# A hybrid decoder trunk on one core: the planner's model of DMA queue and landings, larger transposed pieces of the latents, and four staging sets at attention's end

## The chip, the cores and the metric

The kernel runs on one core of a Trainium2 chip. The core has a matrix engine (TensorE, called PE in the profile; its weight loads, PEld, run beside the matmuls), a vector engine (DVE), a scalar engine (ACT), GpSimd (POOL) and a sync engine (SP). Each engine works through its own instructions in the order in which they stand in the program, and waits at an instruction until its operands are there. Here SP and POOL issue the transfers, each in order, and sixteen DMA engines move the data. The metric is device time in microseconds (us), lower is better.

## What is computed

Two layers over 2048 tokens of 1024 channels: a Mamba-2 mixer, then multi-head latent attention (MLA) with 16 heads, each with a residual, and a last norm over the rows.

```python
def reference(x, positions, ...):
    h = x + mamba2_mixer(rms_norm(x, g_pre[0]), ...)
    cos, sin = rope_tables(positions)
    ckv, k_rope = split(rms_norm(h, kv_g_in) @ kv_w_down, [256])
    k_nope, v = split(rms_norm(ckv, kv_g_latent) @ kv_w_up)
    cq, gate = split(rms_norm(h, g_pre[1]) @ mla_w_in, [384])
    q = rms_norm(cq, mla_g_q) @ mla_w_uq
    o = causal_block_attention(q_nope, rope(q_rope), k_nope, rope(k_rope), v)
    h = h + (o * silu(gate)) @ mla_w_out
    return rms_norm(h, g_final)
```

`ckv` and `cq` are the latents: 256 key-value and 384 query numbers per token, normed and projected up again.

## The kernel before

Tokens are worked in four blocks of 512 (TB), channels in slices of 128 (KD = 8 of them in 1024). Operands of a product are split into two fp16 halves, high and low, and each product is three matmuls into the same PSUM bank (`mm3`, L904 to L906: high by high, high by low, low by high); only the first block of the Mamba layer works in fp32 forms. A "split" below is the pair of instructions that makes the halves: ACT writes the high half, DVE the low one.

**Stage 1, both layers' projections (`layers`, 0 to about 1930 us).** The Mamba layer goes through four blocks of four groups each: input projections, scan, output projection. The MLA part goes block by block through the latents (`mla_kv_down`, `mla_cq`), the gate (`mla_gate`) and the up-projections (`mla_up`), and beside that prepares the next block's normed input xT (`prep16`), by DMA transposes out of a split tile (xT<-wsp). All instructions of this stage are first recorded by a `Score` and then put in order by its planner, `plan`: `forward` simulates the engines, taking at each moment the ready instruction of highest rank; `backward` works out from that schedule how late each may start, which gives the next ranks. This is repeated PLANS times, the shortest schedule is kept, and `play` emits the instructions in the order of their planned starts. All of them so carry one line in the profile, L878. For a DMA the planner has a time of issue and a time to landing (`cost`); for copies the old `forward` also keeps a clock of the transfers in flight (`dma`) and adds LATE, while a transposing DMA lands in a flat 3300 ns and does not hold that clock. The plan fixes order only; real waits are on semaphores. Since DVE, ACT and SP are in order, an instruction whose operand lands late holds whatever stands behind it.

**The latents.** `latent` evicts the product's four banks (128 tokens each) into xs and norms them; `turned` splits each into yt and has SP transpose it in pieces of 128 channels, high and low half together (128x2x128): two pieces per 128 tokens for the key-value latents, into tiles BC, three for the query latents, into tiles yT. DVE then scales each channel slice (BC<-BC, yT<-yT) for the up-projections. The scaling of xT by xg is of the same kind.

**Stage 2, attention (`heads`, about 1930 to 2612 us).** 64 pieces n = 0 to 63, four query blocks in each of the 16 heads. `Pace`, a second planner with its own costs and tables of ranks, orders softmax and products. At its end it starts on the output projection of the first token block: for channel slice k, step G loads attention output, gate and reciprocal row sums into one of GATED staging sets (four DMAs), H multiplies them on DVE, I (ACT) and J (DVE, L2327) make the two halves, and P is the product. ASKED says at which n which slices are loaded.

**Stage 3, the output stage (`back`, 2612 us to the end).** The rest of the output projection, ordered by the framework's scheduler. For block b and slice k, `gated` loads the same three operands into a buffer "os" (three of them), DVE multiplies (L2260, L2262), ACT and DVE split the product into oT (L2466, L2467), and PE multiplies it by W. Products are added to the residual rows h (L2481); when a half block's rows are complete, `final` norms them, scales them by the final gain gf (four instructions of L2487) and writes them out.

## Time and profile before

| | us |
|---|---|
| median of 3 runs | 2784.39 (2779.01 to 2787.86) |
| the profiled execution | 2791.74 |
| its span in the trace | 2789.9 |
| PE's last matmul ends | 2781.0 |

The profile is of one execution, so sums of its durations are made against 2791.74 us, and the span is what its timeline shows. A row of a timeline gives start, length, engine, line, operation, output and inputs, how many like instructions it groups, and in brackets how long the engine stood idle before it and what ended that. A view of waits adds such idle times up by pair. "Granted clock" is the share of full speed that PE was allowed.

### The profile page before, as it was taken

To read this page: it belongs to the slowest core of one execution; us is meant where nothing else is said; L and a number is where in the kernel's file an instruction comes from. 1 tells how busy PE (TensorE), PEld (TensorE's weight loads), DVE (VectorE), ACT (ScalarE), POOL (GpSimd) and SP (SyncE) were. 2 spreads that over 40 slices of the span, in tenths; PEclk is the share of its full clock that TensorE was granted. 3 is DMA by queue.
4 is the path that set the end of the run, shared out by engine and by line. 5 is a ranking of instruction groups with operands and counts; after the bars stand their busy time and mean duration, and the time that the engine had idled before them with its cause. 6 is when DMAs were issued, how large, how long until landed. Compare 5 with 4: busy or idle time off the path is not lost. (4 is left out here: it accounts for less than half of the span.)

```text
span 2789.9 us, 48569 instructions
## 1 busy us (share of the span) xinstructions
PE 2737.9 (98%) x16120; PEld 1550.7 (56%) x16120; DVE 2220.0 (80%) x5048; ACT 1864.2 (67%) x4914; POOL 675.6 (24%) x832
## 2 busy tenths in 40 slices
PE   7999999999999999999999999999999999999998
PEld 6888766554555555555555545454555555555443
DVE  5889899999988879888786564646889888889676
ACT  6889877877776667666655453334888888888322
POOL 0000000000000000000002121324888888888200
PEclk9999999999999999999999999999999999999999
DMA  5333456768668655586567987976999999999894
GB/s 178 98 113 105 118 178 220 215 204 256 187 187 256 175 141 178 160 243 185 145 186 232 292 236 210 250 197 183 181 189 183 186 203 198 190 200 185 209 278 153
DMA packets 687904, 535.88 MB, mean 192 GB/s; under 512 B 496642, under 2 KB 538626, under 8 KB 687652
## 3 DMA queue, kind: packets, MB, share of 16 engines
q1 hardware_dynamic: 674500, 490.16, 69.4%
q0 software_dynamic: 13152, 42.61, 5.1%
q8 instruction: 127, 2.08, 0.3%
q14 instruction: 125, 1.02, 0.1%
HBM read 307.57 MB, written 108.66 MB: 149 GB/s over the span
## 5 line engine op out<-in xcount | busy, mean ns | idle before, releaser
L878 PE MATMUL ps<-xT,wsp 128*128 128x512 f16 (+2 forms) x2416 | 567.7, 386 | 8.7 <-DVE wsp L878 6.0
L878 PE MATMUL ps<-wsp,xT 128*128 128x512 f16 (+3 forms) x2304 | 464.4, 358 | 1.9 <-DVE Sp L878 1.2
L2356 ACT ACTIVATE Pr<-ps,nm 128x512 f32<-128x512 f32 (+3 forms) x640 | 394.5, 628 | 83.7 <-DVE nm L2351 78.1
L2345 DVE TENSOR_REDUCE mx<-ps 128x1 f32<-128x512 f32 (+3 forms) x640 | 366.4, 604 | 54.1 <-PE ps L2311 45.9
L878 PEld LDWEIGHTS <-wsp 128*128 128x128 f16 x2448 | 234.0, 98 | 281.2 <-issue 21.6
L2362 POOL TENSOR_TENSOR HL<-Pr,HL 128x512 f16<-128x512 f32 x320 | 372.6, 1164 | 25.6
L878 PE MATMUL ps<-wsp,yT 128*128 128x512 f16 (+1 forms) x1536 | 356.7, 385 | 1.0 <-DVE rb L878 0.6
L878 POOL DMA_DIRECT2D gate_d<-xs x24 | 13.8, 590 | 1115.4 <-DVE kn L878 1101.3
L878 PEld LDWEIGHTS <-xT 128*128 128x128 f16 x1920 | 185.7, 98 | 166.5 <-issue 6.2
L904 PE MATMUL ps<-K,xT 96*128 96x512 f16 (+3 forms) x640 | 223.0, 348 | 2.9 <-ACT Pr L2356 1.8
L906 PE MATMUL ps<-K,xT 96*128 96x512 f16 (+3 forms) x640 | 221.9, 347 | 0.0
L905 PE MATMUL ps<-K,xT 96*128 96x512 f16 (+3 forms) x640 | 221.8, 347 | 0.0
L2361 POOL CAST HL<-Pr 128x512 f16<-128x512 f32 x320 | 196.6, 614 | 91.7 <-ACT Pr L2356 91.5
L878 DVE SCALAR_TENSOR_TENSOR cacc<-craw,pack,cacc 128x512 f32<-128x512 f32 x288 | 211.4, 746 | 4.6 <-ACT cacc L878 4.1
L878 PEld LDWEIGHTS <-yT 128*128 128x128 f16 x1152 | 110.2, 98 | 129.2 <-issue 3.8
L878 ACT ACTIVATE big<-big,d_cum 128x128 f32<-128x128 f32 x512 | 168.5, 393 | 8.8 <-DMA big<-cumT 8.8
L878 PE MATMUL ps<-xT,st 128*128 128x512 f16 x672 | 154.8, 382 | 3.7 <-DMA st<-w_d 3.7
L2375 ACT ACTIVATE PH<-ps 128x512 f16<-128x512 f32 (+3 forms) x320 | 143.4, 484 | 14.1 <-PE ps L2370 13.3
L2397 PE MATMUL ps<-PX,xT 128*64 128x512 f16 (+1 forms) x640 | 146.2, 383 | 1.6 <-DMA PX<-HL 1.2
L2397 PEld LDWEIGHTS <-xT 128*128 128x128 f16 (+1 forms) x1280 | 95.4, 103 | 91.4 <-issue 15.4
L2356 ACT ACTIVATION_READ_ACCUMULATOR Pr<-ps,nm 128x1 f32 x640 | 133.8, 209 | 0.0
L2370 PE MATMUL ps<-pack,Pr 128*128 128x128 f32 x896 | 133.4, 274 | 0.3 <-ACT Pr L2356 0.3
(380 smaller groups left out, 5348.3 us busy)
## 6 DMA issues: line engine op xcount, KB each, us to landing
wsp<-w_d SPq DMA_DIRECT2D x68, 512.0 KB, 3.9
wraw<-in_ssm_w_in_dram SPq DMA_DIRECT2D x128, 256.0 KB, 3.2
big<-cumT SPq DMA_DIRECT2D x64, 512.0 KB, 4.2
wraw<-in_ssm_w_out_dram SPq DMA_DIRECT2D x64, 256.0 KB, 3.3
w_d<-wsp SPq DMA_DIRECT2D x32, 512.0 KB, 4.3
wsp<-wo_d SPq DMA_DIRECT2D x32, 512.0 KB, 4.3
st<-w_d SPq DMA_DIRECT2D x56, 256.0 KB, 3.7
wsp<-wu_d SPq DMA_DIRECT2D x28, 512.0 KB, 4.2
```

The costliest lines, as they stand in the source:

```text
L878: call(*[self.real(x) for x in args], **{k: self.real(x) for k, x in named.items()})
L904: mm(out, l_hi, r_hi, start=start, stop=False)
L905: mm(out, l_hi, r_lo, start=False, stop=False)
L906: mm(out, l_lo, r_hi, start=False, stop=stop)
L2345: v.tensor_reduce(m[:, at:at + 1], s, AX.X, ALU.max, negate=True)
L2356: nc.scalar.activation(tile("Pr", n, j, c)[:, :w], bank("S", n, j, c)[:, :w], AF.Exp, bias=moves[(4 * n + j) % len(moves)], accum_out=sums ...
L2361: nc.gpsimd.tensor_copy(u[:, 0], x)
L2362: nc.gpsimd.tensor_tensor(u[:, 1], x, u[:, 0], ALU.subtract)
L2370: nc.tensor.transpose(bank("T", n, k)[:, j * P:(j + 1) * P], tile("Pr", n, j, k // 4)[:, k % 4 * P:(k % 4 + 1) * P], self.ident)
L2375: nc.scalar.activation(tile("PH", n, k)[:, c], bank("T", n, k)[:, c], AF.Copy)
L2397: nc.tensor.matmul(o, weights, half(n, k, low), start=start, stop=not left[n][at[0]])
```

## The change

Three groups of edits.

*The planner of stage 1.* A DMA now has a time on the wire (`wires`), a transposing one too, and all of them take turns on it: for copies 102 ns + bytes/359, for transposes 545 ns + bytes/288; a landing is the later of the DMA's own time (2000 ns + bytes/276; 2470 ns + bytes/276) and of the queue's, plus LATE, now 600 ns. `backward` models the wire as well and adds FAR. With EARLY, no DMA of SP starts in the plan more than 30 us before the latest start that the plan before gave it. PLANS goes from 12 to 16.

*The latents.* `turned` now transposes two channel slices at once (128x4x128): one piece per 128 tokens for the key-value latents, into a yT tile; two for the query latents, one of two slices (yT) and one of one (BC). SP's instructions go from 1670 to 1638.

*Attention's end and the output stage.* `Pace` has four staging sets; the two new ones lie in space of K[0] and of two held tiles that earlier heads have left. It asks for slices 0 and 1 at n = 62 and for 2 to 6 at n = 63 (slices from 4 on wait for a free set), and assumes 7500 ns from G to H. `back` has five os buffers.

```diff
--- before.py
+++ after.py
@@ -46,4 +46,4 @@
 DMA_DELAY = 3800
-GATED = 2
-ASKED = {61: (0,), 62: (1,), 63: (2, 3, 4, 5, 6)}
+GATED = 4
+ASKED = {62: (0, 1), 63: (2, 3, 4, 5, 6)}
 TURNED = ((), (0,), (0, 1), (0, 1))
@@ -255,3 +255,3 @@
             else:
-                self.at(self.now + 5500, lambda k: self.ready["DVE"].append(("H", k, 0)), k)
+                self.at(self.now + 7500, lambda k: self.ready["DVE"].append(("H", k, 0)), k)
 
@@ -462,3 +462,4 @@
 ONE = {"mm": "ps", "tr": "ps"}
-PLANS = 12
+PLANS = 16
+EARLY = 30000
 
@@ -525,3 +526,3 @@
     def __init__(self, nc, blank, name):
-        self.ops, self.owns, self.rings = [], [], {}
+        self.ops, self.owns, self.rings, self.wires = [], [], {}, {}
         self.blank, self.name = blank, name
@@ -582,5 +583,6 @@
             if named.get("transpose"):
-                return 1400, 3300
-            issue = 700 if engine == "POOL" else 400
-            return issue, -moved
+                self.wires[len(self.ops)] = 545 + moved / 288
+                return 1300, 2470 + moved / 276
+            self.wires[len(self.ops)] = 102 + moved / 359
+            return 700 if engine == "POOL" else 400, 2000 + moved / 276
         if engine == "PE":
@@ -694,6 +696,6 @@
 
-    SLACK, LATE = dict(DVE=40, ACT=40), 1000
+    SLACK, LATE, FAR = dict(DVE=40, ACT=40), 600, 1800
     HEAR = dict(PE=52, DVE=36, ACT=36, POOL=90, SP=60)
 
-    def forward(self, rank, order):
+    def forward(self, rank, order, due):
 
@@ -701,3 +703,3 @@
         left = [len(p) + len(u) for p, u in zip(preds, uses)]
-        est = [0.0] * len(ops)
+        est = [max(0.0, due + rank[n] - EARLY) if o[0] == "SP" else 0.0 for n, o in enumerate(ops)]
         start = [0.0] * len(ops)
@@ -732,3 +734,4 @@
             if not k:
-                heapq.heappush(waiting[ops[n][0]], (0.0, n))
+                heapq.heappush(waiting[ops[n][0]], (est[n], n))
+                heapq.heappush(events, (est[n], ops[n][0]))
         for o in order:
@@ -760,5 +763,5 @@
                 free[e] = t + step
-            if took < 0:
-                dma = max(dma, t) - took / 260
-                took = max(dma, t + 1900 - took / 160) - t + self.LATE
+            if n in self.wires:
+                dma = max(dma, t + 500) + self.wires[n]
+                took = max(took, dma + 1690 - t) + self.LATE
             if e == "SP":
@@ -796,2 +799,3 @@
         events = []
+        wire = 0.0
         for n, k in enumerate(left):
@@ -813,11 +817,12 @@
             step = ops[n][6]
-            back[n] = t
             free[e] = t + step
             heapq.heappush(events, (t + step, e))
+            if n in self.wires:
+                wire = max(wire + self.wires[n], t)
+                t = max(t, wire)
+            back[n] = t
             for m, full in preds[n].items():
                 f, _, _, _, _, _, step_m, took_m = ops[m]
-                if took_m < 0:
-                    took_m = 2400 - took_m / 150
-                elif f == "SP":
-                    took_m += 800
+                if m in self.wires:
+                    took_m += self.FAR
                 at = t + step + (took_m + self.HEAR[e] - step_m if full else 0)
@@ -838,5 +843,5 @@
         order = sorted(self.owns, key=lambda o: o.first)
-        best = None
+        best, due = None, 0.0
         for i in range(PLANS):
-            made = self.forward(rank, order)
+            made = self.forward(rank, order, due)
             if made is None:
@@ -851,2 +856,3 @@
             rank = [-(b + o[6]) for b, o in zip(back, ops)]
+            due = end if i > 1 else 0.0
             if i > 1:
@@ -2061,6 +2067,7 @@
 
-    def turned(self, raw, f, n, tag):
+    def turned(self, raw, f, n):
 
         nc = self.nc
-        out = [self.t(self.sp, tag, [P, 4, 2, P], F16, bufs=4) for _ in range(n)]
+        sets = [(k, m, self.t(self.sp, "yT" if m == 2 else "BC", [P, 4, 2 * m, P], F16, bufs=4))
+                for k, m in ((0, 2), (2, 1))[:n - 1]]
         for i, x in enumerate(raw):
@@ -2070,5 +2077,5 @@
             nc.vector.scalar_tensor_tensor(u[:, :, 1], y, r, u[:, :, 0], ALU.mult, ALU.subtract)
-            for k in range(n):
-                nc.sync.dma_start(out[k][:, i], u[:, k].rearrange("p s c -> p (s c)"), transpose=True)
-        return out
+            for k, m, o in sets:
+                nc.sync.dma_start(o[:, i], u[:, k:k + m].rearrange("p k s c -> p (k s c)"), transpose=True)
+        return [o[:, :, 2 * j:2 * j + 2] for k, m, o in sets for j in range(m)]
 
@@ -2080,3 +2087,3 @@
         yield
-        self.cV = self.turned(raw, f, 2, "BC")
+        self.cV = self.turned(raw, f, 2)
         self.cT = [self.t(self.sp, "BC", [P, 4, 2, P], F16, bufs=4) for _ in range(2)]
@@ -2098,3 +2105,3 @@
         yield
-        self.qT += self.turned(raw, f, 3, "yT")
+        self.qT += self.turned(raw, f, 3)
         for k in range(3):
@@ -2267,3 +2274,8 @@
             self.W = [self.t(self.wo, f"W{k}", [P, 2, 2, TB], F16, bufs=1) for k in range(KD)]
-            self.staged = [self.t(self.wo, f"os{k}", [P, 3, TB], bufs=1) for k in range(GATED)]
+            staged = [self.t(self.wo, f"os{k}", [P, 3, TB], bufs=1) for k in range(2)]
+            staged = [[s[:, i] for i in range(3)] for s in staged]
+            free = [self.K[0][:, i // 2, i % 2 * 1024:i % 2 * 1024 + 1024] for i in range(4)]
+            free += [self.held(i)[:, 2 * j:2 * j + 2].rearrange("p a b -> p (a b)") for i in (3, 4) for j in range(2)]
+            free = [x.bitcast(F32) for x in free]
+            self.staged = staged + [free[0:3], free[4:7]]
             places = [self.K[0][:, 2 + i // 2, i % 2 * 1024:i % 2 * 1024 + 1024].rearrange(
@@ -2313,4 +2325,3 @@
         def staged(k):
-            s = self.staged[slot[("st", k)]]
-            return s[:, 0], s[:, 1], s[:, 2]
+            return self.staged[slot[("st", k)]]
 
@@ -2460,3 +2471,3 @@
 
-                s = self.t(sp, "os", [P, 3, TB], bufs=3)
+                s = self.t(sp, "os", [P, 3, TB], bufs=5)
                 o, gt, rb = (s[:, i] for i in range(3))
```

What the planner makes of it, at three places of stage 1. The first is SP's queue near its start, from its ninth instruction on, before; hx and hs are rows of x, wraw raw weights:

```order
L878 DMA wraw_158<-in_ssm_w_in_dram 128x2x128
L878 DMA hs_160<-in_x_dram 128x1024
L878 DMA hs_169<-in_x_dram 128x1024
L878 DMA hs_182<-in_x_dram 128x1024
L878 DMA hs_202<-in_x_dram 128x1024
L878 DMA hx_214<-in_x_dram 128x1024
L878 DMA hx_223<-in_x_dram 128x1024
L878 DMA hx_228<-in_x_dram 128x1024
L878 DMA hx_236<-in_x_dram 128x1024
L878 DMA wraw_251<-in_ssm_w_in_dram 128x2x128
```

and after, from the same place:

```order
L884 DMA wraw_158<-in_ssm_w_in_dram 128x2x128
L884 DMA wraw_229<-in_ssm_w_in_dram 128x2x128
L884 DMA wraw_255<-in_ssm_w_in_dram 128x2x128
L884 DMA wraw_276<-in_ssm_w_in_dram 128x2x128
L884 DMA wraw_292<-in_ssm_w_in_dram 128x2x128
L884 DMA wraw_312<-in_ssm_w_in_dram 128x2x128
L884 DMA wraw_346<-in_ssm_w_in_dram 128x2x128
```

The eight loads of x, 512 KB each, have left this place; they stand some fifty rows further down, and the weights follow one another.

The second is DVE in the MLA part, where it scales the next block's xT (128x4x256) by xg. The rows that read a ps tile empty a PSUM bank. Before:

```order
L878 TENSOR_SCALAR xT_17407<-xT_17407,xg_117 128x4x256 x2
L878 TENSOR_REDUCE kn_17706<-kn_17706 128x1
L878 TENSOR_SCALAR xT_17407<-xT_17407,xg_117 128x4x256
L878 TENSOR_SCALAR kn_17706<-kn_17706 128x1
L878 TENSOR_SCALAR xT_17407<-xT_17407,xg_117 128x4x256
L878 TENSOR_SCALAR xT_17515<-xT_17515,xg_117 128x4x256
L878 TENSOR_SCALAR e_119<-kn_17706 128x1
L878 SCALAR_TENSOR_TENSOR yT_17740<-ps_17628,qk,yT_17740 128x512
L878 TENSOR_SCALAR xT_17515<-xT_17515,xg_117 128x4x256
L878 SCALAR_TENSOR_TENSOR xs_17747<-xs_17747,ps_17451 128x512
L878 SCALAR_TENSOR_TENSOR Xp_17752<-ps_17649,qk,Xp_17752 128x512
```

and after:

```order
L884 TENSOR_SCALAR xT_17288<-xT_17288,xg_117 128x4x256
L884 SCALAR_TENSOR_TENSOR big_17507<-ps_17491,qk,big_17507 128x512
L884 TENSOR_SCALAR xT_17288<-xT_17288,xg_117 128x4x256
L884 TENSOR_SCALAR xT_17302<-xT_17302,xg_117 128x4x256
L884 SCALAR_TENSOR_TENSOR yT_17526<-ps_17505,qk,yT_17526 128x512
L884 TENSOR_SCALAR xT_17288<-xT_17288,xg_117 128x4x256
L884 TENSOR_SCALAR xT_17302<-xT_17302,xg_117 128x4x256
L884 TENSOR_SCALAR xT_17288<-xT_17288,xg_117 128x4x256
L884 TENSOR_SCALAR xT_17302<-xT_17302,xg_117 128x4x256 x2
L884 SCALAR_TENSOR_TENSOR Xp_17560<-ps_17524,qk,Xp_17560 128x512
```

Before, five scalings stood ahead of the first emptied bank (yT<-ps); now evictions stand between them.

The third is DVE where the first block's key-value latents are scaled (BC<-) for the up-projection. hs<-ps rows empty the banks of Mamba's last output projection, yt rows are the low halves of latents ahead of their transposition, and the rs rows are steps of a norm. Before:

```order
L878 SCALAR_TENSOR_TENSOR hs_13794<-ps_17025,rr_16744,hs_13794 128x512
L878 SCALAR_TENSOR_TENSOR rsy_17100<-rsq_17091,rsy_17083 128x4
L878 TENSOR_SCALAR e_119<-e_119 128x1
L878 TENSOR_SCALAR BC_17104<-BC_16915,xg_121 128x1024
L878 TENSOR_TENSOR rss_17109<-rsy_17100 128x4
L878 SCALAR_TENSOR_TENSOR hs_13842<-ps_17038,rr_16744,hs_13842 128x512
L878 TENSOR_SCALAR BC_17116<-BC_16926,xg_121 128x1024
L878 SCALAR_TENSOR_TENSOR hs_13855<-ps_17052,rr_16744,hs_13855 128x512
```

and after:

```order
L884 SCALAR_TENSOR_TENSOR hs_14222<-ps_16950,rr_16644,hs_14222 128x512
L884 SCALAR_TENSOR_TENSOR yt_17013<-xs_16766,x_3045_16835,yt_17013 128x2x128
L884 SCALAR_TENSOR_TENSOR rsy_17029<-rsq_17019,rsy_16991 128x4
L884 TENSOR_TENSOR rss_17034<-rsy_17029 128x4
L884 SCALAR_TENSOR_TENSOR rsq_17037<-rsx_16945,rss_17034 128x4
L884 SCALAR_TENSOR_TENSOR hs_14245<-ps_16963,rr_16644,hs_14245 128x512
L884 SCALAR_TENSOR_TENSOR rsy_17044<-rsq_17037,rsy_17029 128x4
L884 TENSOR_SCALAR x_3090_17049<-rsy_17044 128x4
L884 SCALAR_TENSOR_TENSOR hs_14273<-ps_17007,rr_16644,hs_14273 128x512
L884 SCALAR_TENSOR_TENSOR yt_17052<-xs_16873,x_3090_17049,yt_17052 128x3x128
L884 TENSOR_SCALAR BC_17057<-yT_16927,xg_121 128x1024
L884 TENSOR_SCALAR BC_17061<-yT_16927,xg_121 128x1024
```

On PE, six matmuls into the bank of the last hs row (ps_17052 before, ps_17007 after) stand in both just ahead of the first product that reads the scaled BC. Before, both scalings stood ahead of that bank's eviction; now they stand behind it and behind the split yt_17052 of the query latents. The transposition that the scaling needs last is that of yt_17013, and 18 matmuls stand on PE between the end of bank ps_16950, whose eviction stands ahead of yt_17013, and that product.

## The prediction

> **What bounds the kernel now.** I read the busy times first, then who makes TensorE wait, then TensorE's idle time and clock by stage, and last, at each long gap, the timeline of the engine named.
>
> ```profile
> PE 2737.9 (98%) x16120; PEld 1550.7 (56%) x16120; DVE 2220.0 (80%) x5048; ACT 1864.2 (67%) x4914; POOL 675.6 (24%) x832
> ```
>
> TensorE (PE) is the bound. The change adds and removes no matmul, so PE's 2737.9 us stay but for the part spent at half clock. At stake is its idle time, and the waits say who ends it (engine, tile and line, what it waited for: us in total, times, longest):
>
> ```profile
> PE ps L878 <- DVE wsp L878: 6.0, 2, 4.1
> PE ps L904 <- ACT oT L2466: 5.9, 2, 4.1
> PE ps L878 <- DVE yT L878: 4.5, 1, 4.5
> PE ps L878 <- DMA st<-w_d: 3.7, 1, 3.7
> PE ps L878 <- ACT wsp L878: 2.6, 2, 1.7
> PE ps L906 <- DVE xT L2327: 2.0, 1, 2.0
> ```
>
> These are a handful of single events. By stage (columns: stretch in us, its length, then busy time of PE, weight loads, DVE, ACT and POOL, each with its count, then PE's clock, DMA share, GB/s):
>
> ```profile
> 0.00:46.00 46.00, 30.66 (x125) 23.02 (x125) 24.38 (x82) 23.45 (x62) 0.20 (x4) 0.89 0.60 202
> 46.00:1560.00 1514.00, 1513.00 (x9022) 883.05 (x9021) 1286.22 (x2784) 1080.78 (x2823) 25.02 (x37) 1.00 0.63 182
> 1560.00:1810.00 250.00, 236.64 (x1210) 119.04 (x1209) 143.26 (x329) 110.93 (x198) 63.37 (x94) 0.98 0.87 239
> 2630.00:2760.00 130.00, 123.82 (x567) 55.32 (x565) 93.05 (x166) 31.23 (x56) 0.00 (x0) 0.99 0.86 258
> ```
>
> Length less PE gives the idle time: 15.3 us at the start, 1.0 in 1514 us of Mamba, 13.4 in the latent attention's projections (MLA), 6.2 in the output stage. Several gaps leave a second cost, PE at half clock:
>
> ```profile
> 29.20:36.00 6.80, 5.09 (x12) 4.07 (x13) 3.97 (x15) 0.82 (x3) 0.00 (x0) 0.50 0.31 71
> 1568.60:1572.00 3.40, 3.40 (x9) 1.19 (x9) 3.40 (x7) 0.69 (x2) 2.65 (x4) 0.50 1.02 333
> 1800.70:1807.50 6.80, 5.82 (x14) 2.09 (x15) 6.10 (x13) 1.38 (x2) 2.02 (x4) 0.50 0.89 268
> 2585.80:2589.20 3.40, 3.32 (x10) 1.71 (x10) 2.17 (x7) 2.42 (x9) 1.68 (x2) 0.50 1.04 224
> 2667.70:2671.10 3.40, 2.93 (x7) 1.00 (x8) 1.77 (x3) 1.05 (x2) 0.00 (x0) 0.50 1.04 260
> 1659.00:1663.00 4.00, 3.43 (x16) 1.56 (x16) 3.93 (x7) 1.10 (x1) 0.90 (x1) 1.00 1.08 358
> ```
>
> Half of the busy time at 0.50 is lost: 2.5, 1.7, 2.9, 1.7 and 1.5 us. Four of the five stretches lie at gaps of 3.7 to 4.5 us; the gap of 1.87 us at 1659.6 left the clock at 1.00.
>
> **Part 1, the start (planner).**
>
> ```profile
> 7.32 2.82 SPq L878 DMA_DIRECT2D hs<-in_x_dram  x4
> 10.57 2.95 SPq L878 DMA_DIRECT2D hx<-in_x_dram  x4
> ```
> ```profile
> 30.43 0.42 DVE L878 TENSOR_TENSOR wsp<-wraw,wsp 128x256 fp32r<-128x256 f32 x1
> 30.91 5.38 PE L878 MATMUL ps<-xT,wsp 128*128 128x512 f32 x12 [4.10 <-DVE wsp L878]
> 33.14 0.42 ACT L878 ACTIVATE wsp<-wraw 128x256 fp32r<-128x256 f32 x1 [5.93 <-DMA wraw<-in_ssm_w_in_dram]
> ```
>
> Eight loads of x that only the next token blocks need go to the queue at 7.3 to 13.5 us, ahead of weights for which ACT then waits 5.93 us; and DVE makes the low half that releases PE at 30.91 only after a chain of small steps on the time step dt. EARLY moves those x loads behind some fifty others, and the new DVE order puts the splits between the chain's steps. The gap of 4.10 us, the two on ACT's wsp (2.6 in the waits) and 2.5 us of half clock, 9.2 us, are open to this. The first x loads and the first transposition, which make the rest of the 15.3 us, come as before. DVE has the same chain to do, so I take **8**.
>
> **Part 2, MLA.** Here the in-order engines stand behind landings:
>
> ```profile
> ACT yt L878 <- DMA hs<-h_d: 30.2, 4, 11.1
> DVE yT L878 <- DMA yT<-yt: 15.0, 8, 4.1
> ```
> ```profile
> 1554.49 10.62 SPq L878 DMA_TRANSPOSE xT<-wsp  x4
> 1565.55 0.88 DVE L878 TENSOR_SCALAR xT<-xT,xg 128x1024 f16<-128x1024 f16 x2 [5.80 <-DMA xT<-wsp]
> 1567.72 0.74 DVE L878 SCALAR_TENSOR_TENSOR yT<-ps,qk,yT 128x512 f16<-128x512 f32 x1
> 1568.52 0.96 PE L878 MATMUL ps<-yT,wsp 128*128 128x512 f16 x2 [4.46 <-DVE yT L878]
> ```
>
> DVE waits 5.80 us for transposed pieces, scales five at once, and only then empties the PSUM bank that PE needs: 4.46 us. The old planner let a transposition land in a fixed time without holding the queue; now it takes queue time and 600 ns more, so the plan issues it earlier and (in the order rows shown with the change) empties banks between the scalings. 32 of 1016 queue instructions go as well; at the 1.2 us of issue in the row below that is 38 us of SP's time, off PE's path. The stretch holds 13.4 us of idle PE and 1.7 + 2.9 us at half clock, 18 us. The gaps of 4.46, 3.67 and 1.87 us and their clock, 14.6, follow from such waits; the 3.4 us left are small waits on evictions, which I keep. I take **14.5**.
>
> **A wait that the change adds.** For the first block's key-value latents the new order puts the scaling BC<-yT behind the eviction of the very last bank that PE fills before it needs BC, and behind a split for the query latents. Before, that eviction stood behind both scalings, and PE lost nothing. Durations, from the trace of before:
>
> ```profile
> 1485.68 0.46 DVE L878 SCALAR_TENSOR_TENSOR yt<-xs,x,yt 128x256 f16<-128x256 f32 x1
> 1492.46 0.48 DVE L878 TENSOR_SCALAR BC<-BC,xg 128x1024 f16<-128x1024 f16 x1
> 1493.38 0.75 DVE L878 SCALAR_TENSOR_TENSOR hs<-ps,rr,hs 128x512 f32<-128x512 f32 x1 [0.38 <-PE ps L878]
> ```
> ```profile
> L878 SPq DMA_TRANSPOSE BC<-yt x32: 1173/1231/2028, 1475.9 to 1851.2; - x32
> DMA to landing us min/median/max: 2.3/2.9/3.9
> ```
>
> By DVE's order: eviction 0.75, a split of 384 columns (0.46 for 256, so some 0.6), scaling 0.48, and about 0.2 to hear of each other: 2.0 us. By the transposition: the last piece is made behind the eviction one group earlier, 18 matmuls before PE is through, each 0.22 us (the row at 1659.57 below: nine in 2.10), so 3.9 us; 0.75 + 0.46 + 0.2 and a landing of 2.9 to 3.9 put the data 0.4 to 1.4 us after that end, and PE starts 0.6 later. The later of the two counts: 2.0, and 3 with a landing of 4.9, a microsecond past the longest of the row; and 0 if another engine holds PE there anyway. A gap of that size left the clock alone at 1659.6, so I add none and take **−2.5**. Behind the waiting scaling stand only DVE's next evictions, whose banks PE does not need before it.
>
> The Trainium skill ("TensorE: Matmul & The Clock Gate", the section on HAM oscillation) has as its abstract rule that PE gaps should not exceed about 3.4 us. The trace agrees on the four long gaps and on 1659.6; the stretch at 2585.8, where PE is busy 3.32 of 3.40 us and the waits list no gap of that length, does not fit. By the rule the new stall costs no clock; were it to cost the 1.7 us of the 1568.6 row, the sum would be 1.7 us less.
>
> ```profile
> 1659.57 2.10 PE L878 MATMUL ps<-yT,wsp 128*128 128x512 f16 x9 [1.87 <-DVE big L878]
> ```
>
> The Trainium skill ("DMA: Bandwidth & Descriptors", the section on latency and other measured facts) gives transposing DMAs 261 GB/s. An estimate from that page: a merged piece of 128 KB takes 0.25 us longer than one of 64 KB. No row here isolates a 128 KB piece; the stall by it would stay at DVE's 2.0.
>
> **Part 3, Mamba.** Loads start at most 30 us before the plan needs them, and LATE falls from 1000 to 600 ns: less cover.
>
> ```profile
> ACT wsp L878 <- DMA wraw<-in_ssm_w_in_dram: 21.3, 18, 3.8
> ```
>
> Between 348 and 700 us ACT waits 18 times for weights, 1.2 us each, and PE (1.0 us idle in the whole stage) hides it: ACT and DVE run ahead of PE by the weight buffers. In the two orders, counted in matmuls at the trace's own pace, the loads with under 4.5 us of PE work between their place and their first user's rise from 65 to 109 in Mamba. If cover fails, the loss is 44 × 1.2 = 53 us; if it holds, 0. The near row is the 18 hidden waits: **−2**.
>
> **Part 4, attention's end.** Only the order around the last two query blocks of the last head differs.
>
> ```profile
> 2607.91 0.39 PE L906 MATMUL ps<-W,xT 128*128 128x512 f16 x1 [2.03 <-DVE xT L2327]
> ```
>
> PE waits 2.03 us for the low half of the gated operand of projection slice 7, which the old order takes fourth; with four staging sets the slices come 0 to 7 and this one last. 2.03 us and 1.7 at 2585.8 are open. But the gate multiplications of slices 2 and 3 now stand ahead of six low-half splits on DVE, and a late load there holds all of them. From +3.7 to the rival's −3.5; I take **+1.5**.
>
> **Part 5, output stage.**
>
> ```profile
> 2660.72 4.87 DVE L2487 SCALAR_TENSOR_TENSOR h<-h,rsy,gf 128x1024 f32<-128x1024 f32 x4
> 2665.50 1.29 DVE L2260 TENSOR_TENSOR os<-os 128x512 f32<-128x512 f32 x2
> 2667.49 1.29 ACT L2466 ACTIVATE oT<-os 128x512 f16<-128x512 f32 x2 [7.68 <-DVE os L2262]
> 2668.17 0.61 PE L904 MATMUL ps<-W,oT 128*128 128x512 f16 x1 [4.07 <-ACT oT L2466]
> ```
>
> DVE scales four finished rows by the final gain (4.87 us) ahead of the gates of slices 6 and 7, with three buffers for gated operands; PE waits 4.07 us and loses 1.5 to the clock, and 1.82 + 0.29 in block 3. With five buffers the new order has slice 6 done and slice 7 multiplied before that scaling, with only slice 7's low half behind it, and block 3's eight gates ahead of block 2's second half. Open: 7.7. Slice 7's low half still stands behind the scaling. With DVE no further ahead of PE than before, the five steps of slices 6 and 7 that now go first, 0.65 each and some 3.3 in all, push the scaling to 2664.0; the low half is there at 2669.6; PE, free at 2664.1, comes to it after slice 6's twelve matmuls and two more, at 2667.2, and waits 2.4, too short for the clock. That leaves **+5** (7.7 if five buffers let DVE run ahead, 2 if block 3 alone gains).
>
> **Sum.** 8 + 14.5 − 2.5 − 2 + 1.5 + 5 = **24.5 us**. Against the profiled execution's 2791.74 us that is 2767; it ran 7.4 above the median of the runs shown, with the same instructions, so against 2784.39 it is **2760**.
>
> **Rivals.** *The queue, not the plan.* DMA share is 0.87 in MLA's stretch and 1.02 at its worst gap. If the transposed pieces are late because the engines are full, no order helps there: 8 − 2.5 + 1.5 + 5 − 2 = 10, **2774**. Against it: DVE came for the pieces (1565.55 less 5.80) 5.3 us after the first was issued, while issuing the four took 10.62.
>
> *Attention's end stalls.* The loads for slices 2 and 3 land late and DVE stands: after about five slices' products, 3.2 us of PE work, PE waits 1.8 and the clock takes 1.7: −3.5 where I have +1.5, **2765**.
>
> *Thinner cover is paid in part.* PE sees four tenths of Mamba's 53 us, 21, and most is given back: 24.5 + 2 − 21 = 5.5, **2779**.
>
> *Slower.* ACT, at 71% in Mamba, no longer runs ahead: all 44 loads' 1.2 us fall on PE, 53 us against 26.5 of gain, **2811**. It decides from 22 such waits on; PE's 1.0 us in 1514 speaks against it.
>
> **Chances.** Forecast 0.58 (2748 to 2769), queue 0.22, attention's end 0.07, paid in part 0.07, slower 0.06. A measurement tells about 0.3% (8.4 us) from no change, so faster is below 2776: 0.58 + 0.07 + 0.15 of the queue case (its gain may be 14 or 5), 0.80; slower, above 2793, 0.06; the rest 0.14. The range goes from nearly all idle time regained and no new stall (2744) to the partly paid case and a little past it (2781); some 0.1 stay out.
>
> **What would show it.** Start: no PE gap over 2 us after 26 us. MLA: no wait of 4 us on yT or st; one new gap near 2 us, released by DVE BC, before the first key up-projection of block 0. Mamba: PE idle below 3 us, more ACT waits on wraw. Attention: no wait on L2327's successor. Output: no 4 us gap on oT. Wrong if MLA's gaps stay at other places, or Mamba's idle exceeds 10 us.

## The result and the profile after

The changed kernel takes **2767.6 us** (median of 5, 2759.55 to 2770.36); the kernel before, now with 5 runs, 2785.82 (2779.01 to 2790.42). The ratio is 0.9931, with a 95% interval of 0.9909 to 0.9952: about 19 us less, where 24.5 were forecast. The profiled executions differ by more, 24.1 us in their spans (2789.9 before, 2765.8 after), since that of before was one of its slower ones.

Who makes TensorE (PE) wait in the changed kernel (us in total, times, longest):

```profile
PE ps L884 <- DMA hx<-in_x_dram: 5.1, 1, 5.1
PE ps L884 <- DMA st<-w_d: 4.5, 1, 4.5
PE ps L2408 <- DMA PX<-HL: 3.3, 2, 2.9
PE ps L884 <- DVE BC L884: 1.9, 1, 1.9
PE ps L884 <- DMA wsp<-wu_d: 1.8, 1, 1.8
PE ps L910 <- DVE Xp L884: 1.3, 1, 1.3
```

The waits on splits (DVE's and ACT's wsp), yT and oT, which led the list of before, are gone but for 0.8 us. The wait for weights (st, 3.7 us before) stands at another place, and one of 2.9 us for transposed probabilities (PX) and the one on BC have come. By stage, with the columns of the prediction (length, busy PE, weight loads, DVE, ACT, POOL, then PE's clock, DMA share, GB/s), the changed kernel:

```profile
0.00:46.00 46.00, 39.07 (x170) 31.18 (x171) 30.27 (x93) 32.71 (x86) 0.20 (x4) 0.96 0.48 142
46.00:1440.00 1394.00, 1394.00 (x8404) 818.71 (x8403) 1206.32 (x2588) 1020.74 (x2689) 0.70 (x1) 1.00 0.61 178
1440.00:1910.00 470.00, 461.46 (x2394) 234.31 (x2392) 265.02 (x611) 202.90 (x378) 114.52 (x168) 0.99 0.86 240
1910.00:2602.00 692.00, 683.61 (x4441) 395.48 (x4440) 606.02 (x1541) 571.98 (x1692) 557.77 (x659) 1.00 0.99 190
2602.00:2757.00 155.00, 154.90 (x718) 70.03 (x716) 104.68 (x204) 36.47 (x67) 0.00 (x0) 1.00 0.79 232
```

and the kernel before, in the two stretches that the prediction cut otherwise (MLA from 1440 us, attention):

```profile
1440.00:1930.00 490.00, 476.64 (x2488) 241.96 (x2487) 269.15 (x622) 208.44 (x392) 115.88 (x170) 0.99 0.81 229
1930.00:2618.00 688.00, 680.80 (x4427) 394.46 (x4426) 604.60 (x1536) 571.46 (x1690) 558.77 (x658) 1.00 1.00 189
```

Length less busy PE is the idle time: at the start 6.9 us (15.3 before), in Mamba 0 (1.0), in MLA 8.5 (13.4), in attention 8.4 (7.2), in the output stage 0.1 (6.2). Half-clock stretches of the changed kernel, which are fewer too (that at 14.2 us has its like before, from 15.5 to 18.9):

```profile
14.20:17.60 3.40, 3.40 (x10) 1.88 (x9) 3.36 (x9) 3.40 (x10) 0.00 (x0) 0.50 0.15 40
1649.20:1652.60 3.40, 3.40 (x9) 1.22 (x8) 0.00 (x0) 0.00 (x0) 0.00 (x0) 0.50 1.01 94
1789.10:1792.50 3.40, 3.40 (x10) 1.19 (x9) 3.39 (x7) 1.95 (x3) 1.24 (x2) 0.50 1.05 339
2591.20:2594.60 3.40, 3.15 (x8) 1.19 (x9) 1.80 (x4) 0.63 (x1) 0.00 (x0) 0.51 0.80 187
```

At the start, SP's queue (columns: start, length, engine, line, operation, tile, how many):

```profile
1.19 1.85 SPq L884 DMA_DIRECT2D hx<-in_x_dram  x4
3.09 31.60 SPq L884 DMA_DIRECT2D wraw<-in_ssm_w_in_dram  x15
```

Weights follow the first x loads without the eight other x loads between them. And the predicted new wait, on DVE and PE:

```profile
1483.62 0.75 DVE L884 SCALAR_TENSOR_TENSOR hs<-ps,rr,hs 128x512 f32<-128x512 f32 x1 [0.27 <-PE ps L884]
1484.29 0.61 DVE L884 SCALAR_TENSOR_TENSOR yt<-xs,x,yt 128x384 f16<-128x384 f32 x1
1484.82 0.88 DVE L884 TENSOR_SCALAR BC<-yT,xg 128x1024 f16<-128x1024 f16 x2
```
```profile
1485.44 0.81 PE L884 MATMUL ps<-BC,wsp 128*128 128x512 f16 x3 [1.86 <-DVE BC L884]
```

Eviction 0.75, split 0.61, first scaling: after the eviction DVE waits for nothing, so it is DVE's order that makes the 1.86 us, not the transposition's landing.

### The profile page after: what moved, and what is told of

Its sections match the earlier page's. It is cut to its first block, busy times and chain, and to the rows that moved or that the text cites. A ratio compares the mean times of both kernels' runs of the same rounds, so it can differ in the third digit from the quotient of the medians.

```text
span 2765.8 us, 48506 instructions
## 1 busy us (share of the span) xinstructions
PE 2733.0 (99%) x16120; PEld 1549.7 (56%) x16120; DVE 2215.8 (80%) x5048; ACT 1866.2 (67%) x4914; POOL 673.2 (24%) x832
## 4 chain that ended last, share of the span: by engine, by line
PE 95%; DMA 2%; DVE 1%; SPq 1%; ACT 1%; POOL 0%; issue 0%; POOLq 0%; ACTq 0%; DVEq 0%
PE ps L884 66%; PE ps L2408 7%; PE ps L910 6%; PE ps L911 6%; PE ps L912 6%; PE ps L2381 3%; SPq L884 1%; DMA st<-w_d 1%; DVE mx L2356 1%; PE ps L2323 0%; DMA hs<-h_d 0%; DMA PX<-HL 0%; DMA xT<-wsp 0%; POOL HL L2373 0%; ACT Pr L2367 0%
## 5 line engine op out<-in xcount | busy, mean ns | idle before, releaser
L884 PE MATMUL ps<-wsp,yT 128*128 128x512 f16 (+1 forms) x1728 | 399.3, 384 | 0.0
L884 POOL DMA_DIRECT2D gate_d<-xs x24 | 13.4, 557 | 1130.1 <-DVE xs L884 1126.2
L884 PEld LDWEIGHTS <-yT 128*128 128x128 f16 x1344 | 129.1, 98 | 151.1 <-issue 3.5
```

Of the source, the lines that this page charges most:

```text
L884: call(*[self.real(x) for x in args], **{k: self.real(x) for k, x in named.items()})
```

## The experiments

Each ratio below is to the kernel before, timed on the same chip, with its 95% interval. The next table holds PE's idle time by stage, in one profiled execution of each kernel, length less busy PE as above; MLA runs from 1440 us to attention's first product. The last column says how far that one execution's time lay from the kernel's median, in us: a column of idle times is read with it.

| kernel | ratio (95%) | start | MLA | attention | output | profiled less median |
|---|---|---|---|---|---|---|
| before | 1 | 15.3 | 13.4 | 7.2 | 6.2 | +5.9 |
| changed | 0.9931 (0.9909 to 0.9952) | 6.9 | 8.5 | 8.4 | 0.1 | 0.0 |
| plan_only | 0.9959 (0.9944 to 0.9974) | 7.6 | 18.6 | 6.5 | 5.5 | +4.3 |
| plan_l650 | 0.9989 (0.9973 to 1.0004) | 7.1 | 11.4 | 5.7 | 5.6 | −12.5 |
| turn_only | 1.0047 (1.0032 to 1.0063) | 14.5 | 23.7 | 6.4 | 5.2 | +5.3 |
| turn_l1050 | 1.0008 (0.9995 to 1.0021) | 15.2 | 17.7 | 6.2 | 6.4 | +10.8 |
| pace_only | 0.9976 (0.9959 to 0.9993) | 15.6 | 11.8 | 7.2 | 2.3 | +5.7 |
| end_old | 0.9942 (0.9922 to 0.9962) | 7.7 | 5.7 | 6.3 | 4.6 | −9.1 |
| os3 | 0.9930 (0.9910 to 0.9950) | 8.2 | 8.7 | 7.2 | 1.4 | −1.7 |
| asked_61 | 0.9931 (0.9919 to 0.9943) | 8.5 | 13.7 | 7.3 | 0.0 | +5.9 |
| no_early | 0.9940 (0.9927 to 0.9954) | 10.7 | 11.7 | 6.2 | 0.0 | +0.3 |
| late650 | 0.9952 (0.9934 to 0.9969) | 8.5 | 22.3 | 9.7 | 0.0 | +14.6 |
| far5000 | 0.9961 (0.9949 to 0.9972) | 9.7 | 6.7 | 7.9 | 0.0 | −6.9 |
| wire | 0.9986 (0.9977 to 0.9996) | 8.0 | 24.6 | 8.0 | 0.0 | +4.5 |

Two things are read from it at once. The start's and the output stage's columns fall into two groups each, and the group follows one group of edits. MLA's column does not: end_old, os3, asked_61 and the changed kernel have the same order there and stand between 5.7 and 13.7. The executions with the most idle time there (wire, turn_only, late650) also lay 4.5 to 14.6 us above their medians, so that column tells of an execution as much as of an order.

**The planner alone.** The kernel before with all edits of the `Score`, and nothing else (EARLY's line stands for them):

```diff
-        est = [0.0] * len(ops)
+        est = [max(0.0, due + rank[n] - EARLY) if o[0] == "SP" else 0.0 for n, o in enumerate(ops)]
```

> The kernel before with the planner's edits alone (PLANS, EARLY, the wire model, LATE, FAR). My theory: the planner gave the start's 10.9 us and most of what MLA lost of its idle time, and the output stage gave the other 7.7. Then this takes 15 to 18 us off the kernel before (about 2769): PE idle in the first 46 us near 7 us, no idle in Mamba, one gap of 1.6 to 1.9 us ahead of the first product that reads BC, and the output stage's gaps of about 4 and 2 us on oT still there. Rival (the merged transpositions relieved the queue in MLA): the start's 11 us alone come off, about 2775, and MLA's idle PE stays at 13 us.

Measured 0.9959, some 11 us. The start came down as expected and the wait on BC is there (1.6 us). But MLA's idle time rose, by waits like these:

```profile
PE ps L884 <- DVE xT L884: 10.1, 2, 9.2
PE ps L884 <- DMA wsp<-w_d: 6.9, 2, 5.4
```

So the planner's edits by themselves gave the start, and in this execution nothing in MLA: my theory fell there, and the time is near the rival's. The rival's reason, that the merge relieved the queue, is for the next kernel.

**The merged pieces alone**, with the old planner; the edit is that of `turned` and its two callers.

```diff
-            for k in range(n):
-                nc.sync.dma_start(out[k][:, i], u[:, k].rearrange("p s c -> p (s c)"), transpose=True)
+            for k, m, o in sets:
+                nc.sync.dma_start(o[:, i], u[:, k:k + m].rearrange("p k s c -> p (k s c)"), transpose=True)
```

> The kernel before with the merged latent transpositions alone, planned by the old planner. My theory: the merge itself is worth nothing or costs the wait on BC, which here stands behind the eviction of the last bank without a split between (0.75 + 0.15 + 0.48 + 0.2, about 1.6 us): within 4 us of the kernel before, 2782 to 2790, and the start's and the output stage's gaps as before. Rival (32 transpositions fewer unload the queue): MLA's idle PE falls from 13.4 to under 7 us, and with its clock the time is near 2777.

Measured 1.0047, 13 us slower: outside both. The start and the output stage are as before; MLA lost, with 4.0 us on BC and waits on st (12.4 us in two) and wsp. That two parts each left MLA worse than before, and both together better, asked whether a planned order is more than one throw. Three kernels test it, with an edit of LATE that means nothing. The first is turn_only again:

```diff
-    SLACK, LATE = dict(DVE=40, ACT=40), 1000
+    SLACK, LATE = dict(DVE=40, ACT=40), 1050
```

> The merged pieces with the old planner again, with LATE at 1050 in place of 1000 ns, also without meaning. If the old planner places merged pieces badly by its model (a flat 3300 ns for every transposition, no time on the queue), this is slower than the kernel before again, by 8 to 18 us, with waits of 4 us and more on BC, wsp or st in MLA. If turn_only's 13 us were one schedule's bad luck, this is within 6 us of the kernel before.

Measured 1.0008: 11 us of the 13 were one order's. The other two are on the planner's side, 650 for 600 ns, with the whole change and with the planner alone:

> The changed kernel with LATE at 650 in place of 600 ns, a change without meaning that makes the planner choose another schedule. It measures how much of the result is the one schedule's luck. If the planner's model is what counts, the time is within 4 us of 2767 and MLA's idle PE (with its half clock) is between 6 and 14 us. If the schedule chosen by chance counts, it is 6 us or more off, either way.

> The planner's edits alone again, with LATE at 650 in place of 600 ns, a change without meaning. plan_only was at 0.9959 of the kernel before. If single pieces of 64 KB make the new planner's schedules worse, this is no faster than 0.996, with 15 us or more of idle PE and half clock in MLA. If plan_only was one schedule's bad luck, it may reach 0.993, with the start's 8 us of idle PE in both cases.

Measured 0.9952 and 0.9989: 6 and 8 us slower than the same kernels at 600. The 6 are within the two intervals and between the two forecasts; the 8 are at their edge. plan_l650's time is what its first reading named, single pieces that do badly; but orders with merged pieces scatter as far (wire, far5000), so it does not show that. In late650's profile, of an execution 14.6 us above its median, two waits on st make 15.4 us:

```profile
PE ps L884 <- DMA st<-w_d: 15.4, 2, 9.0
PE ps L884 <- DMA hx<-in_x_dram: 6.3, 2, 5.5
PE ps L884 <- DVE xs L884: 5.0, 1, 5.0
```

So 50 ns in the planner's cost moved the median by 6, 8 and 11 us. Executions of one order differ as well: plan_l650 ran from 2775.7 to 2792.34 us, and its profile, with 11.4 us of idle PE in MLA, is of the execution at 2775.7. What the merge is worth lies within these.

**Three edits of the planner's numbers** on the changed kernel: EARLY so large that it never holds a load back (`EARLY = 1e9`), transposes longer on the wire, and all loads ranked earlier:

```diff
-                self.wires[len(self.ops)] = 545 + moved / 288
+                self.wires[len(self.ops)] = 545 + moved / 120
```

> The changed kernel with EARLY set so large that it never holds a load back; the wire model, LATE, FAR and the merged pieces stay. My theory: EARLY is what freed the start (the eight x loads return to the ninth place of SP's queue and the splits wait for weights again), so PE's idle time in the first 46 us returns from 7 to some 14 us, with 2.5 us at half clock: 2774 to 2778, and MLA stays within 4 us of the changed kernel. Rival A: the wire model alone orders the start well enough, and the time stays within 3 us of 2767. Rival B: early loads also crowd MLA's queue, and MLA's idle time returns to 13 us or more: 2782 and above.

> The changed kernel with a longer time on the wire for transposes in the planner: 545 ns + bytes/120 in place of bytes/288, which is 2.7 us for a piece of 256 KB, about what a piece took to issue back to back in MLA (10.62 us for four before). My theory: MLA's remaining waits on st and wsp (4.5 and 1.8 us, and two times 1.7 us of half clock) come from transposes that hold SP's queue longer than planned; planned longer, these waits shrink to under 3 us in all: 2758 to 2764, and the wait of about 1.9 us on BC stays. Rival (MLA's DMA engines are full, or it is a matter of each execution): the waits only move, 2764 to 2772. If the longer plan costs order elsewhere, slower than 2772.

> The changed kernel with FAR at 5000 in place of 1800 ns, so that every load is ranked 3.2 us earlier. If MLA's waits on st and wsp come from loads that are ordered too late by a few us, its idle PE with half clock (13.6 us in the changed kernel's profile, 5.7 and 15.2 in two others of the same order) falls to that of BC alone, under 6 us, and the time to 2760 or below. Rival: these loads stand in queues that are full whatever their order, so this is one more schedule among others, 2766 to 2784, with single waits of 4 us and more on st, wsp or xT.

Without EARLY the eight x loads return to SP's ninth place and the start's idle time goes from 6.9 to 10.7 us, not to 14: the gap of 4.1 us stays away, so the rest of the start is the doing of the planner's other edits, which were not taken apart. The time, 0.9940, cannot be told from the changed kernel's. Longer wires made it slower, 0.9986: against my theory, outside its rival, and the third case that was named, a longer plan that costs order elsewhere. FAR at 5000 has little idle time in MLA in its profile, which is of an execution 6.9 us below the median; the median is 2777.13 (0.9961). Neither a longer wire nor a longer lead shortened MLA reliably. Where the changed kernel waits 4.5 us for st, SP's queue shows:

```profile
1631.47 3.55 SPq L884 DMA_TRANSPOSE xT<-wsp  x1
1635.12 3.70 SPq L884 DMA_DIRECT2D st<-w_d  x2
1638.87 8.40 SPq L884 DMA_TRANSPOSE xT<-wsp  x1
1647.32 1.05 SPq L884 DMA_DIRECT2D Xd<-in_mla_w_out_dram  x2
```
```profile
1635.00:1650.00 15.00, 10.47 (x48) 4.53 (x46) 8.93 (x14) 1.87 (x2) 2.50 (x3) 0.97 1.13 198
```

The two st loads were issued by 1638.8, and PE got the one it needed at 1649.07, over 10 us later, with the DMA engines at a share of 1.13 and only 198 GB/s. Landings of the xT pieces (least, median, most) in MLA did not get shorter, and DVE's waits for them (total, times, longest) add up to the same; before:

```profile
DMA to landing us min/median/max: 3.7/6.6/13.5
DVE xT L878 <- DMA xT<-wsp: 12.3, 3, 5.8
```

and after:

```profile
DMA to landing us min/median/max: 3.1/6.9/14.9
DVE xT L884 <- DMA xT<-wsp: 12.3, 3, 6.8
```

What did change is that no wait of PE in MLA follows from DVE's waits for them any more; the loads between the transposes are what comes late. DVE's waits for the latents' own pieces (yT) shrank, from 15.0 us in 8 to 3.0 in 3, and are at most 2.8 in the other seven kernels with both planner and merge; with one of the two they are 0.8 to 12.1. PE's idle time in MLA did not follow them.

What fills the engines at that wait is open. From 1630 to 1650 us POOL's queue (q0) held more of their time than SP's (q1), which has the transposes and the weights (packets, MB, share of the 16 engines):

```profile
q0 software_dynamic: 897, 2.92, 61.7%
q1 hardware_dynamic: 2230, 1.69, 47.7%
```

So POOL's writes (v_d, wo_d and others, 256 KB each) are as good a suspect as the transposes; no run took either away.

**Attention's end and the output stage.** The changed kernel with two staging sets again, and with three os buffers again:

```diff
-GATED = 4
-ASKED = {62: (0, 1), 63: (2, 3, 4, 5, 6)}
+GATED = 2
+ASKED = {61: (0,), 62: (1,), 63: (2, 3, 4, 5, 6)}
```
```diff
-                s = self.t(sp, "os", [P, 3, TB], bufs=5)
+                s = self.t(sp, "os", [P, 3, TB], bufs=3)
```

> The changed kernel with attention's end undone (two staging sets, slices asked for at 61, 62 and 63, 5500 ns from G to H); the five os buffers of the output stage stay. My theory: the four sets only exchange one wait for another, so the wait on PX<-HL of 2.9 us with its half clock goes and the one on the low half of slice 7 (about 2 us with half clock near 2586) comes back: within 3 us of the changed kernel, 2765 to 2770, and PE idle after the output stage's start stays near 0. Rival A: the four sets are what freed the output stage: its gap of 4 us on oT returns, about 2774. Rival B: the four sets cost, and this is 4 us faster, about 2763.

> The changed kernel with three os buffers in the output stage. My theory: the two added buffers gave the 7.7 us of that stage, so its waits on oT return (about 4 and 2 us, 1.5 us of half clock) and the time rises by 6 to 8 us, to about 2775. Rival: the output stage gained because it starts differently (slices 0 to 6 already multiplied, other DMA load), and the time stays within 2 us of 2768.

With two sets the time is 0.9942 (some 3 us more, within the intervals), and the waits on oT return although the buffers are five:

```profile
PE ps L910 <- ACT oT L2473: 3.0, 2, 1.9
PE ps L912 <- DVE oT L2474: 1.5, 1, 1.5
```

With three buffers and four sets one wait of 1.3 us returns, and the time does not move. So it is not the buffers; the profiles are rival A's, though the time of end_old alone would not tell, and I had credited the wrong edit. Four sets on the kernel before, alone:

> The kernel before with attention's end alone changed (four staging sets, slices 0 and 1 asked for at 62, 7500 ns); the output stage keeps three buffers, the planner and the pieces are the old ones. My theory, from the runs so far: the four sets empty the output stage of its idle time (8.3 us with the half clock before) and cost 2 to 4 us in attention's end, so this is 4 to 6 us faster than the kernel before, ratio 0.998 to 0.9985, with no wait on oT above 1.5 us. Rival: the output stage is emptied only together with five buffers, and the time is within 2 us of the kernel before, or slower by the 3 us of attention's end.

Measured 0.9976, 6.7 us faster, as expected, with one wait of 1.9 us on oT left. How it works shows in the last low halves of block 0's gated operands on DVE (first and last start behind the durations), and in attention's last products on PE, before:

```profile
L2327 DVE TENSOR_TENSOR xT<-os,xT x2: 692/1161/1630, 2606.2 to 2631.8; 128x512 f16<-128x512 f32 x2
L2397 PE MATMUL ps<-PX,xT x640: 376/379/404, 1949.9 to 2615.0; 128*128 128x512 f16 x80, 128*64 128x512 f16 x80
L2467 DVE TENSOR_TENSOR oT<-os,oT x24: 681/692/693, 2642.8 to 2743.6; 128x512 f16<-128x512 f32 x24
```

and after:

```profile
L2338 DVE TENSOR_TENSOR xT<-xT,xT x1: 691/691/691, 2605.6 to 2605.6; 128x512 f16<-128x512 f32 x1
L2408 PE MATMUL ps<-PX,xT x640: 376/379/634, 1933.4 to 2599.0; 128*128 128x512 f16 x80, 128*64 128x512 f16 x80
L2478 DVE TENSOR_TENSOR oT<-os,oT x24: 681/691/693, 2620.2 to 2718.0; 128x512 f16<-128x512 f32 x24
```

Block 0's last low half was started 16.8 us after attention's last PX product, and now starts 6.6 us after it; the first low half of block 1 (oT) follows 21.2 instead of 27.8 us after it. DVE so stays ahead of PE through the whole output stage. The same two distances, with PE's idle time in the output stage, go by the staging sets in all five kernels, and not by the buffers:

| kernel | staging sets | os buffers | last low half | first oT | PE idle |
|---|---|---|---|---|---|
| before | 2 | 3 | 16.8 | 27.8 | 6.2 |
| end_old | 2 | 5 | 15.8 | 27.0 | 4.6 |
| pace_only | 4 | 3 | 6.6 | 20.7 | 2.3 |
| os3 | 4 | 3 | 6.7 | 20.0 | 1.4 |
| changed | 4 | 5 | 6.6 | 21.2 | 0.1 |

The rows of end_old, the one with five buffers and two sets:

```profile
L2334 DVE TENSOR_TENSOR xT<-os,xT x2: 691/1158/1624, 2578.5 to 2603.0; 128x512 f16<-128x512 f32 x2
L2404 PE MATMUL ps<-PX,xT x640: 376/379/404, 1925.6 to 2587.2; 128*128 128x512 f16 x80, 128*64 128x512 f16 x80
L2474 DVE TENSOR_TENSOR oT<-os,oT x24: 681/692/693, 2614.2 to 2713.5; 128x512 f16<-128x512 f32 x24
```

The price, a wait on PX<-HL at attention's end, was tried with slices 0 and 1 asked for at 61 (`ASKED = {61: (0, 1), 63: (2, 3, 4, 5, 6)}`):

> The changed kernel with slices 0 and 1 asked for at n = 61 in place of 62. If the wait on PX<-HL at attention's end (2.9 and 2.0 us in two runs, with 1.6 us of half clock) comes from the staging loads standing between the last transposes on SP, it shrinks to under 1 us and the time falls by 2 to 4 us, to 2763 to 2765, with the output stage still without waits. Rival: the last transposes wait for the DMA engines in any case, and the time stays within 2 us of the changed kernel.

That wait goes, one of 1.65 us on DVE comes, with half clock behind it again, and the time is the same. No kernel tried beats the changed one by what can be measured.

## Why the prediction was right, and where it was not

The sign and the range held, and 24.5 us were forecast for 18 to 19. Term by term, in the profiled executions, idle time and half clock together (half of the busy time at 0.50, as in the prediction):

| term | forecast | profiles |
|---|---|---|
| start | +8 | 8.4 less idle, 2.5 less half clock: +10.9 |
| Mamba | −2 | +1.0 |
| MLA with the wait on BC | +12 | 4.9 and 1.2: +6.1 |
| attention's end | +1.5 | −1.2 and 0.1: −1.1 |
| output stage | +5 | 6.1 and 1.5: +7.6 |
| sum | 24.5 | 24.5 |

The equal sums are chance: MLA gave half of what was taken for it, and the start and the output stage gave more. In the medians it is less, 18 to 19. The gaps were read in an execution of the kernel before that lay 7.4 us above the median shown, and the whole 24.5 were then taken off that median; part of those gaps may be that execution's own, which is not shown.

**Start: right.** 2.5 of the 10.9 us are in the first x loads and the first transposition, which I had left out as unchanged. All nine kernels with the new planner and EARLY at 30000 have 6.9 to 9.7 us of idle PE there, the four with the old one 14.5 to 15.6. This is the planner's one gain that every order repeats.

**The new wait on BC: right,** place, cause and size (2.5 taken, 2.0 by DVE's order, 1.86 measured, and 1.9 in os3, end_old, late650 and asked_61). It left the clock alone, as taken.

**MLA: the step that failed.** I took 14.5 us because the three long gaps "follow from such waits" and the new plan has none of them; the profiles gave 6.1. Only the gap of 4.46 us was shown to stand behind DVE's wait for transposed pieces. That of 3.67 was a load of weights itself, issued on SP at 1793.9 us between transposes, so no order of DVE's scalings would have removed it (PE's timeline, before):

```profile
1801.68 4.02 PE L878 MATMUL ps<-xT,st 128*128 128x512 f16 x9 [3.67 <-DMA st<-w_d]
```

Waits of that kind come back at other places, 4.5 us on st and 1.8 on wsp, which is what the prediction itself had named as its sign of being wrong. The same order gave 5.7 to 13.7 us of idle PE in four executions; orders that differ by 50 ns of a cost gave 22.3 (late650), 11.4 and 18.6 (the two of the planner alone), each in one execution. The rival "the queue, not the plan" was nearer on the reason: the pieces' landings were no shorter in the new order (a median of 6.9 us for 6.6) nor with longer wires (8.7). The measured time lies between its 2774 and the 2760 forecast. What is left in this term cannot be told from the scatter of orders.

**Output stage: mechanism wrong, size near.** I argued from five buffers; by os3 they are worth no time that shows, and by pace_only and end_old the four sets did it, through block 0's gates. The waiting had its cause one stage earlier than the place where it showed. The 2.4 us that were to stay on slice 7's low half, counted with DVE no further ahead of PE than before, did not come, since DVE was further ahead.

**Attention's end: sign wrong, small.** The wait on slice 7's low half went, and one of 2.9 us on PX<-HL came, with its half clock. The rival there named late gate loads; the new wait was on the transposes of probabilities instead.

**Mamba: nothing lost.** PE was busy 1394.00 us in 1394.00, so the 2 taken off were not paid. But ACT's waits on raw weights, which were to be more, are fewer, 18 from 46 to 1440 us where before there were 22 (24.6 and 26.8 us in all): the cover did not get thinner in a way that shows, and whether PE could have hidden it was not tried.

What adds up in medians: four sets 6.7 us, and the planner alone 3 to 11 by the order it falls on; the merge and the two more buffers are within the scatter. Whether the change's planner is better in MLA than the old one, or this order a good throw, stays open: of the five orders that have the new planner, the merge and the four sets, the changed kernel's had the lowest ratio, with those of no_early and late650 within its interval.

## What to carry to other kernels

When a planner orders in-order queues, change one of its costs by a meaningless amount and time that too; here the answer moved by 6 to 11 us, as much as the edits under test. In a stage whose transfers land late, a removed wait can come back at another place, so its length is no estimate of the gain. Where an engine waits for operands at a stage's start, look first at what their producer still has to finish from the stage before, and only then at buffers.

## What the runs showed of the hardware

Half clock does not need a long gap. In the changed kernel PE was idle 1.81 us here (PE's timeline):

```profile
1787.68 0.61 PE L884 MATMUL ps<-BC,wsp 128*128 128x512 f16 x2 [1.81 <-DMA wsp<-wu_d]
```

and 3.4 us at 0.50 followed from 1789.1; 1.86 us at 1485 left it at full speed, as did 1.87 at 1659.6 before. The prediction left out a stretch of the kernel before, from 15.5 to 18.9 us at 0.50, that lies behind a gap as short:

```profile
15.01 1.07 PE L878 MATMUL ps<-xT,wsp 128*64 128x512 f32 x3 [1.89 <-DVE wsp L878]
```

So gaps of 1.8 to 1.9 us went both ways, and the prediction's "too short for the clock" for one of 2.4 us was not safe. The Trainium skill ("TensorE: Matmul & The Clock Gate", Part 1) has a free-running window of about 3.4 us, which would let equal gaps fare differently by where they fall; no run here moved a gap to test it. The rule of no gap above about 3.4 us that the prediction cited is then not a safe bound, and the trace shows one below 2 us that cost 1.7.

A transposing DMA's issue held SP for 8.40 us, and a load issued ahead of it landed more than 10 us after its issue. Durations of issue in ns (least, median, most) in MLA after:

```profile
L884 SPq DMA_TRANSPOSE xT<-wsp x24: 1231/2494/8405, 1511.4 to 1784.2; - x24
```

The changed planner counts 1300 ns for each.
